# Second half of an out-projection as seven block products for eight, and the first half's last tiles in two sweeps

## The chip, the cores and the metric

The kernel runs on one core of a Trainium2 chip. The metric is the device time of one launch in microseconds (us). Engines are called by their names in the profile: PE is TensorE (PEld its weight loads), DVE is VectorE, ACT is ScalarE, POOL is GpSimd, SP the queue that issues the transfers.

## What is computed

A block of a bidirectional state-space model on 1024 tokens of 1024 channels: norm, in-projection, convolution, a scan over chunks of 128 tokens in both directions, a gate, a norm by groups, and then the out-projection with the residual and a last norm. Only the last lines matter here:

```python
    y = (yg.reshape(b, l, D_INNER) * norm_w.astype(jnp.float32)).astype(u.dtype)   # (1, 1024, 2048)
    return y @ w_out                                                               # w_out (2048, 1024)
...
        h = h + out
    return rmsnorm(h, final_norm_w)
```

All is float32. The kernel makes each float32 product out of three faster matmuls: both operands are split into a high part (rounded to the engine's reduced float32) and a low part (what is left), and high x high, high x low and low x high are added up in PSUM.

## The kernel before

Eight groups of channels go through in-projection and scan one after the other; `y` is written to DRAM (`y_d`), transposed. The out-projection contracts over 2048 channels in two halves of eight k-tiles of 128 channels (`NO` = 8). The first half can begin before the last group's scan has ended: token tiles 0 to 3 (`out_unit(0, t, ...)`) are put between the steps of the last scan, tiles 4 to 7 follow behind it. Its result plus the input x goes to DRAM (`h_d`). The second half then takes the eight token tiles once more, with `h` loaded from `h_d`; then comes the last norm.

For a token tile `out_unit` issues 48 matmuls of 128x512: eight k-tiles, three part products, two halves of the output columns. `out_prep` loads the tile of `y` (tag `th`, two buffers) and of `h` (tag `xc`, three buffers) and splits `y`: high part on ScalarE, low part on VectorE. It stands in the middle of the tile before. `load_wo` loads one row of 128 channels of the weight, 512 KB, into `raw` (tag of the pool `wp`, two buffers), scales it by the norm's weight and splits it in the same two operations (line 520 on ScalarE, 521 on VectorE). The second half's eight rows are loaded between tiles 4 to 7, two behind each, into a pool `op2` that is opened where the scan's pool is closed.

The last tile is computed in three column parts one after the other, so that its norm can begin early.

The order on each engine is set by a scheduler of the tile framework, by priorities that follow the order of the code; each engine then works through its list in that order, and waits where an operand or a buffer is not ready. All transfers here are issued by SP, in the order of its list.

```python
        raw = wp.tile([P, DM], F32, tag="raw", name=f"wo{half}{k}", bufs=2)
        nc.sync.dma_start(out=raw, in_=w_out[:, half * NO + k, :])
...
    for t in range(NC // 2, NC):
        prep = out_unit(0, t, wo1, prep, (0, t + 1) if t < NC - 1 else (1, 0))
        for _ in range(2):
            if len(wo2) % 4 == 0:
                tiles = wo_tiles(op2, 1, len(wo2) // 4)
            wo2.append(load_wo(tiles, 1, len(wo2)))
    for t in range(NC):
        prep = out_unit(1, t, wo2, prep, (1, t + 1) if t < NC - 1 else None)
```

## Time and profile before

| | us |
|---|---|
| median of 3 runs | 983.37 (981.67 to 983.98) |
| the profiled execution, device time | 985.42 |
| its span, first to last instruction | 983.7 |
| TensorE matmuls busy | 945.5 (96%) |
| VectorE busy | 727.9 (74%) |
| ScalarE busy | 539.2 (55%) |

The profile is of one execution. Times in it count from the start of its span. A list of instructions gives for each its start and its length; matmuls are pipelined, so their pace is read from the distance of starts. The first half's tiles 4 to 7 and the second half fill the last 143 us or so. A chain of waits is the work that ended last, followed back from the end.

### The profile page before, as it was taken

Reading aid. Unit: us, or ns where it says so; the run is one execution under the profiler, and the core shown is the slowest. Engines: PE = TensorE matmul, PEld = TensorE weight load, DVE = VectorE, ACT = ScalarE, POOL = GpSimd, SP = SyncE. Lnnn points to the kernel's source line nnn. Section 1 sums busy time; section 2 is a strip of 40 time slices with the busy share of each in tenths; the row PEclk is TensorE's granted clock in tenths of the full one; section 3 lists DMA queues with packets and bytes.
Section 4 is the critical chain, followed back from the end, with each engine's and each line's share of the span. In section 5 each row is a group of like instructions: output and inputs, shape, how many; then the busy total and the mean of one; then the engine's idle time right before and its main releaser. Section 6 shows DMA issues by size and latency. Waiting matters only on the chain.

```text
span 983.7 us, 15133 instructions
## 1 busy us (share of the span) xinstructions
PE 945.5 (96%) x5220; PEld 806.1 (82%) x5220; DVE 727.9 (74%) x1552; ACT 539.2 (55%) x1458; POOL 53.8 (5%) x88
## 2 busy tenths in 40 slices
...
GB/s 223 95 86 97 43 70 94 111 70 70 101 120 53 74 99 124 49 75 98 126 52 82 86 129 63 78 80 126 96 64 142 172 264 174 200 278 142 118 85 65
DMA packets 157325, 107.62 MB, mean 109 GB/s; under 512 B 75248, under 2 KB 133312, under 8 KB 157248
## 3 DMA queue, kind: packets, MB, share of 16 engines
...
## 4 chain that ended last, share of the span: by engine, by line
PE 56%; DVE 12%; DMA 12%; ACT 12%; issue 6%; POOL 2%; SPq 1%; DVEq 0%; POOLq 0%; ACTq 0%
PE po L562 16%; PE ipx L180 12%; PE ipC L180 9%; DMA fb<-rows_d 7%; PE ipB L180 7%; ACT yo L479 3%; DVE x L196 3%; ACT fb L424 2%; PE pz L157 2%; PE pyo L462 2%; PE pyd L468 2%; PE sb L393 2%; ACT fb L419 2%; DVE mt L429 1%; PE sf L393 1%
## 5 line engine op out<-in xcount | busy, mean ns | idle before, releaser
L479 ACT ACTIVATE yo<-pyo,ecs 128x64 f32<-128x64 f32 x448 | 103.1, 320 | 35.8 <-PE pyo L462 30.2
L419 ACT ACTIVATE fb<-fb,cfb 128x128 f32<-128x128 f32 x256 | 85.1, 399 | 55.1 <-DMA fb<-rows_d 49.6
L424 ACT ACTIVATE fb<-fb,cfb 128x128 f32<-128x128 f32 x256 | 84.0, 398 | 3.8 <-DVE fb L421 3.7
L196 DVE SCALAR_TENSOR_TENSOR x<-ipx,prm,x 128x1022 f32<-128x1022 f32 (+1 forms) x64 | 81.1, 1268 | 3.7 <-ACT x L190 3.6
L157 PE MATMUL pz<-wz_1l,uh 128*128 128x256 f32 (+1 forms) x248 | 73.0, 294 | 2.0 <-DVE wz_1l L123 2.0
L157 PE MATMUL pz<-wz_0h,ul 128*128 128x256 f32 (+1 forms) x248 | 73.3, 296 | 0.4 <-DVE ul L301 0.2
L157 PE MATMUL pz<-wz_0l,uh 128*128 128x256 f32 (+1 forms) x248 | 72.0, 290 | 0.0
L157 PE MATMUL pz<-wz_0h,uh 128*128 128x256 f32 (+1 forms) x248 | 71.2, 287 | 0.0
L157 PE MATMUL pz<-wz_1h,ul 128*128 128x256 f32 (+1 forms) x248 | 70.9, 286 | 0.0
L468 PEld LDWEIGHTS pyd<-xb,mt 128*128 128x128 f32 x512 | 66.7, 191 | 4.9 <-DVE mt L429 1.8
L157 PE MATMUL pz<-wz_1h,uh 128*128 128x256 f32 (+1 forms) x248 | 70.4, 284 | 0.0
L471 DVE SCALAR_TENSOR_TENSOR y<-xb,coef,pyd 128x64 f32<-128x64 f32 x256 | 62.5, 273 | 10.5 <-PE pyd L468 10.3
L468 PE MATMUL pyd<-xb,mt 128*128 128x64 f32 x512 | 64.7, 269 | 0.0
L429 DVE TENSOR_TENSOR mt<-fb,pcb 128x512 f32<-128x512 f32 x64 | 43.1, 681 | 15.3 <-PE pcb L427 13.0
L385 DVE TENSOR_TENSOR pb<-pb,sb 128x256 f32<-128x256 f32 x48 | 19.8, 412 | 42.0 <-PE sb L393 41.1
L421 DVE COPY_PREDICATED fb<-trif,fb 128x512 f32<-128x512 uint32 x64 | 47.1, 736 | 3.7 <-ACT fb L419 3.6
L157 PEld LDWEIGHTS pz<-wz_1l,uh 128*128 128x128 f32 x248 | 46.9, 189 | 3.4 <-DVE wz_1l L123 3.2
L157 PEld LDWEIGHTS pz<-wz_0h,ul 128*128 128x128 f32 x248 | 47.2, 190 | 1.3 <-DVE ul L301 1.1
L571 DVE TENSOR_TENSOR h<-po,h 128x1024 f32<-128x1024 f32 (+2 forms) x10 | 10.1, 1011 | 51.3 <-PE po L562 51.3
L157 PEld LDWEIGHTS pz<-wz_0h,uh 128*128 128x128 f32 x248 | 47.1, 190 | 0.5
L157 PEld LDWEIGHTS pz<-wz_0l,uh 128*128 128x128 f32 x248 | 47.1, 190 | 0.0
L157 PEld LDWEIGHTS pz<-wz_1h,ul 128*128 128x128 f32 x248 | 46.9, 189 | 0.2
(511 smaller groups left out, 2667.5 us busy)
## 6 DMA issues: line engine op xcount, KB each, us to landing
fb<-rows_d SPq DMA_DIRECT2D x128, 256.0 KB, 4.3
y_d<-yt SPq DMA_DIRECT2D x256, 32.0 KB, 2.0
wo<-in_ssd_w_out_dram SPq DMA_DIRECT2D x16, 512.0 KB, 4.2
yt<-y_d SPq DMA_DIRECT2D x16, 512.0 KB, 5.1
xt<-in_x_dram SPq DMA_DIRECT2D x8, 512.0 KB, 5.9
h<-in_x_dram SPq DMA_DIRECT2D x8, 512.0 KB, 4.8
h_d<-h SPq DMA_DIRECT2D x8, 512.0 KB, 3.0
h<-h_d SPq DMA_DIRECT2D x8, 512.0 KB, 3.6
```

The source lines that it names most:

```text
L157: nc.tensor.matmul(pz[:, i, 0:m], a[:, k, tok], b, start=at == 0, stop=at == 3 * NK - 1)
L180: nc.tensor.matmul(ps[:, half * 512:(half + 1) * 512], a[:, k, :], b[:, k, :], start=n == 0, stop=n == 3 * NK - 1)
L196: nc.vector.scalar_tensor_tensor(out=acc[:, o], in0=ps[:, i], scalar=w(k), in1=acc[:, o], op0=ALU.mult, op1=ALU.add)
L393: nc.tensor.matmul(ps[:, 0:CW], xb[:, CW:CW + P], xw, start=True, stop=True)
L419: nc.scalar.activation(out=ef[:, h], in_=ef[:, h], func=AF.Identity, bias=cfb[:, 1, c, hsl(g, h)])
L421: nc.vector.copy_predicated(ef, trif.bitcast(U32).unsqueeze(1).broadcast_to([P, HG, P]), fb[:, 0])
L424: nc.scalar.activation(out=ef[:, h], in_=ef[:, h], func=AF.Exp, bias=cfb[:, 0, c, hsl(g, h)])
L429: nc.vector.tensor_tensor(out=mt, in0=ef, in1=pcb[:, 0:P].unsqueeze(1).broadcast_to([P, HG, P]), op=ALU.mult)
L468: nc.tensor.matmul(pyd[:, cs], mt[:, h, :], xb[:, cs], start=True, stop=True)
L471: nc.vector.scalar_tensor_tensor(out=y[:, cs], in0=xb[:, cs], scalar=coef[:, h:h + 1], in1=pyd[:, cs], op0=ALU.mult, op1=ALU.add)
L479: nc.scalar.activation(out=yo[:, cs], in_=pyo[:, d * CW + h * HD:d * CW + (h + 1) * HD], func=AF.Copy, scale=ecs[:, d, c, hsl(g, h)])
L562: nc.tensor.matmul(pos[i], l_, r_[:, cols[i]], start=k == 0 and a == 0, stop=k == NO - 1 and a == 2)
```

## The change

The second half's product is cut into blocks: for a pair of token tiles the left operand is a 2x2 block matrix (two tiles of tokens; the first and the last four k-tiles of the half), and so is the weight (first and last four k-tiles; columns 0 to 511 and 512 to 1023). Winograd's form of Strassen's method gives the 2x2 product of blocks by seven block products in place of eight, with sums of blocks ahead of and behind them. A block product is 12 matmuls of 128x512 (`product`, line 689).

- `weights_a`, `weights_b` and `weights_c` make the seven weight operands: `w11`, `t1`, `t2`, `w21` (a), `w22`, `t3` (b), `t4` (c). `weights_a(k)` and `weights_b(k)` each load the rows k and k + 4 into `raw` and scale them on ScalarE in place (line 600); so each row is loaded twice. The differences are made on VectorE (line 610), the splits by a cast on ScalarE and a difference on VectorE (lines 591 and 592). `weights_c` needs no load.
- `pair_prep` loads both tiles of `y` and of `h` and makes the seven token operands: `a11`, `s1`, `s2`, `a12`, `s3`, `s4`, `a22`.
- `pair_unit` issues the seven products. Some of the sums behind them are made by letting a product go on in an accumulator: ScalarE copies c12 to c11, later c12 to c22 and c22 to c21, and the next products add to the copies. The product s1 x t1 is added to `h` of both tiles by VectorE.
- Tiles 4 to 7 of the first half are computed in two sweeps: all four over the k-tiles 0 to 3, then all four over 4 to 7. After the first sweep the first half's weights of the k-tiles 0 to 3 are no longer needed, and `t3` and `w22` take their place. `weights_a(n)` stands behind the n-th tile of the first sweep, `weights_b(n)` behind the n-th of the second. `x` is loaded in the second sweep (`load_h`).
- The last tile is no longer computed in column parts; its norm's second part is scaled on ScalarE and multiplied by the norm's weight on VectorE behind that.

```diff
+    def load_h(t):
+        h = cp.tile([P, DM], F32, tag="xc", name=f"h0{t}", bufs=3)
+        nc.sync.dma_start(out=h, in_=x[t * P:(t + 1) * P, :])
+        return h
...
-        h = cp.tile([P, DM], F32, tag="xc", name=f"h{half}{t}", bufs=3)
-        nc.sync.dma_start(out=h, in_=(x if half == 0 else h_d)[tok, :])
+        h = load_h(t) if t < NC // 2 else None
...
-        last = half == 1 and t == NC - 1
-        cols = [slice(0, 512), slice(512, 1024)]
-        ka = [(k, a) for k in range(NO) for a in range(3)]
...
+    def split(src, dst):
+        nc.scalar.copy(dst[0], src)
+        nc.vector.tensor_tensor(out=dst[1], in0=src, in1=dst[0].bitcast(F32), op=ALU.subtract)
+    def scaled_rows(k, name):
+        rows = []
+        for n in (k, k + HK):
+            raw = wp.tile([P, DM], F32, tag="raw", name=f"{name}{n}", bufs=2)
+            nc.sync.dma_start(out=raw, in_=w_out[:, NO + n, :])
+            nc.scalar.activation(out=raw, in_=raw, func=AF.Copy,
+                                 scale=prm[:, 192 + NO + n:193 + NO + n])
+            rows += [raw[:, 0:512], raw[:, 512:1024]]
+        return rows
...
+    def temps(name):
+        t_ = cp.tile([P, 2, 512], F32, tag="th", name=name)
+        return t_[:, 0], t_[:, 1]
...
+    def weights_a(k):
...
+        r11, r12, r21, r22 = scaled_rows(k, "wa")
+        d1, d2 = temps(f"da{k}")
+        split(r11, [p_[:, k] for p_ in W["w11"]])
+        minus(d1, r12, r11)
+        split(d1, [p_[:, k] for p_ in W["t1"]])
+        minus(d2, r22, d1)
+        split(d2, [p_[:, k] for p_ in W["t2"]])
+        split(r21, [p_[:, k] for p_ in W["w21"]])
...
+    def weights_b(k):
...
+        r11, r12, r21, r22 = scaled_rows(k, "wb")
+        d3, _ = temps(f"db{k}")
+        split(r22, [p_[:, k] for p_ in W["w22"]])
+        minus(d3, r22, r12)
+        split(d3, [p_[:, k] for p_ in W["t3"]])
...
+    def weights_c(k):
...
+        e, d = temps(f"dc{k}")
+        for o, n in ((e, 0), (d, 1)):
+            minus(o, W["w21"][n][:, k].bitcast(F32), W["t2"][n][:, k].bitcast(F32))
+        nc.vector.tensor_tensor(out=d, in0=d, in1=e, op=ALU.add)
+        split(d, [p_[:, k] for p_ in W["t4"]])
...
+    def pair_prep(i):
+        ys, hs = [], []
+        for t in (2 * i, 2 * i + 1):
+            yt = cp.tile([P, NO, P], F32, tag="th", name=f"yt1{t}")
+            nc.sync.dma_start(out=yt, in_=y_v[:, NO:2 * NO, t * P:(t + 1) * P])
+            ys.append([yt[:, q * HK:(q + 1) * HK].rearrange("p k t -> p (k t)") for q in range(2)])
+        for t in (2 * i, 2 * i + 1):
+            h = cp.tile([P, DM], F32, tag="xc", name=f"h1{t}", bufs=3)
+            nc.sync.dma_start(out=h, in_=h_d[t * P:(t + 1) * P, :])
+            hs.append(h)
...
+        put("a11", a11)
+        s1, s2 = room("a")
+        nc.vector.tensor_tensor(out=s1, in0=a21, in1=a22, op=ALU.add)
+        put("s1", s1)
+        minus(s2, s1, a11)
+        put("s2", s2)
+        put("a12", a12)
+        s3, s4 = room("b")
+        minus(s3, a11, a21)
+        put("s3", s3)
+        minus(s4, a12, s2)
+        put("s4", s4)
+        put("a22", a22)
+        return A, hs
+    def product(ps, a, w, fresh):
+        n = 0
+        for k in range(HK):
+            for l_, r_ in ((a[0], w[0]), (a[0], w[1]), (a[1], w[0])):
+                nc.tensor.matmul(ps, l_[:, k, :], r_[:, k, :], start=fresh and n == 0,
+                                 stop=n == 3 * HK - 1, skip_group_check=True)
+                n += 1
...
+            nc.scalar.activation(out=h[:, HI], in_=h[:, HI], func=AF.Copy, scale=r)
+            nc.vector.tensor_tensor(out=h[:, HI], in0=h[:, HI], in1=fnw[:, HI], op=ALU.mult)
+            nc.sync.dma_start(out=out[t * P:(t + 1) * P, HI], in_=h[:, HI])
...
+    def add(t, h, cs, ps, ss, i):
+        nc.vector.tensor_tensor(out=h[:, cs], in0=ps, in1=h[:, cs], op=ALU.add)
+        nc.scalar.activation(out=ps, in_=h[:, cs], func=AF.Square, accum_out=ss[:, i:i + 1])
+        if i:
+            nc.vector.tensor_tensor(out=ss[:, 0:1], in0=ss[:, 0:1], in1=ss[:, 1:2], op=ALU.add)
...
+    def pair_unit(i, prep, nxt):
+        A, (h1, h2) = prep
+        c1 = ps_ip.tile([P, DM], F32, tag="ip", name=f"po1{i}")
+        c11, c12 = c1[:, LO], c1[:, HI]
+        product(c12, A["a11"], W["w11"], True)
+        nc.scalar.copy(c11, c12)
+        pw = pst(f"p5{i}")
+        product(pw, A["s1"], W["t1"], True)
+        for h in (h1, h2):
+            nc.vector.tensor_tensor(out=h[:, HI], in0=pw, in1=h[:, HI], op=ALU.add)
+        product(c12, A["s2"], W["t2"], False)
+        product(c11, A["a12"], W["w21"], False)
+        nprep = pair_prep(nxt) if nxt is not None else None
+        c2 = ps_ip.tile([P, DM], F32, tag="ip", name=f"po2{i}")
+        c21, c22 = c2[:, LO], c2[:, HI]
+        nc.scalar.copy(c22, c12)
+        ss1, ss2 = (ops.tile([P, 3], F32, tag="ss", name=f"oss{i}_{j}") for j in range(2))
+        add(2 * i, h1, LO, c11, ss1, 0)
+        product(c22, A["s3"], W["t3"], False)
+        product(c12, A["s4"], W["w22"], False)
+        nc.scalar.copy(c21, c22)
+        add(2 * i + 1, h2, HI, c22, ss2, 0)
+        add(2 * i, h1, HI, c12, ss1, 1)
+        product(c21, A["a22"], W["t4"], False)
+        finish(2 * i, h1, ss1, False)
+        add(2 * i + 1, h2, LO, c21, ss2, 1)
+        finish(2 * i + 1, h2, ss2, nxt is None)
+        return nprep
...
+    tiles, pos = list(range(NC // 2, NC)), {}
+    preps = {tiles[0]: prep}
+    for q in range(2):
+        for n, t in enumerate(tiles):
+            if q == 0:
+                if n:
+                    preps[t] = out_prep(0, t)
+                if n < 2:
+                    po = ps_ip.tile([P, DM], F32, tag="ip", name=f"po0{t}")
+                    pos[t] = [po[:, cs] for cs in (LO, HI)]
+                else:
+                    pos[t] = [pst(f"po0{t}_{c}") for c in range(2)]
+            _, yh, yl = preps[t]
+            for k in range(q * HK, (q + 1) * HK):
+                for a in range(3):
+                    for p_, cs in zip(pos[t], (LO, HI)):
+                        nc.tensor.matmul(p_, (yh, yh, yl)[a][:, k, :], wo1[k][(0, 1, 0)[a]][:, cs],
+                                         start=k == 0 and a == 0, stop=k == NO - 1 and a == 2)
+            if q == 0:
+                weights_a(n)
+            else:
+                h = load_h(t)
+                for p_, cs in zip(pos[t], (LO, HI)):
+                    nc.vector.tensor_tensor(out=h[:, cs], in0=p_, in1=h[:, cs], op=ALU.add)
+                nc.sync.dma_start(out=h_d[t * P:(t + 1) * P, :], in_=h)
+                weights_b(n)
...
-    for t in range(NC // 2, NC):
-        prep = out_unit(0, t, wo1, prep, (0, t + 1) if t < NC - 1 else (1, 0))
-        for _ in range(2):
-            if len(wo2) % 4 == 0:
-                tiles = wo_tiles(op2, 1, len(wo2) // 4)
-            wo2.append(load_wo(tiles, 1, len(wo2)))
-    for t in range(NC):
-        prep = out_unit(1, t, wo2, prep, (1, t + 1) if t < NC - 1 else None)
+    prep = pair_prep(0)
+    for k in range(HK):
+        weights_c(k)
+    for i in range(NC // 2):
+        prep = pair_unit(i, prep, i + 1 if i + 1 < NC // 2 else None)
```

How the instructions stand on three engines is shown by pieces of their lists (no times are in them). A name ends in the buffer's number; `wo1h0`, `wo1l0` are the second half's weights of before, high and low part, `po04` is the accumulator of the first half's tile 4, `yh06` the high part of tile 6's `y`.

VectorE, where tile 5's sum is added to `h`, before (line 565 adds, 521 makes a weight's low part, 538 that of `y`):

```order
L521 SCALAR_TENSOR_TENSOR wo1l0_9314<-wo10_9315,prm_74,wo1h0_9313 128x1024 [waits DMAHW3_49,DMAHW2_49,DMAHW4_49,DMAHW1_49,Activation_49]
L521 SCALAR_TENSOR_TENSOR wo1l0_9314<-wo11_9319,prm_74,wo1h0_9313 128x1024 [waits Activation_49]
L565 TENSOR_TENSOR h05_9281<-po05_9323,h05_9281 128x1024 [waits PE_49]
L538 TENSOR_TENSOR yl11_9556<-yt11_9551,yh11_9555 128x1024 [waits DMAHW7_49,Activation_49]
L521 SCALAR_TENSOR_TENSOR wo1l0_9314<-wo12_9382,prm_74,wo1h0_9313 128x1024 [waits DMAHW0_49,Activation_49]
L521 SCALAR_TENSOR_TENSOR wo1l0_9314<-wo13_9386,prm_74,wo1h0_9313 128x1024 [waits DMAHW1_49,Activation_49]
```

and after (774 adds half a tile, 610 and 592 belong to `weights_a(0)` and `(1)`, 542 is the low part of `y`):

```order
L592 TENSOR_TENSOR ow21_9278<-wa4_9282,ow21_9278 128x512 [waits Activation_49]
L774 TENSOR_TENSOR h04_9466<-po04_9250,h04_9466 128x512 [waits PE_49]
L774 TENSOR_TENSOR h04_9466<-po04_9250,h04_9466 128x512
L610 TENSOR_TENSOR da1_9333<-wa1_9327 128x512 [waits Activation_49]
L774 TENSOR_TENSOR h05_9509<-po05_9302,h05_9509 128x512 [waits PE_49]
L592 TENSOR_TENSOR ow11_9275<-wa1_9327,ow11_9275 128x512 [waits Activation_49]
L610 TENSOR_TENSOR da1_9333<-wa5_9330,da1_9333 128x512 [waits DVE_49,Activation_49]
L592 TENSOR_TENSOR ot1_9276<-da1_9333,ot1_9276 128x512 [waits Activation_49]
L592 TENSOR_TENSOR ow21_9278<-wa5_9330,ow21_9278 128x512 [waits Activation_49]
L592 TENSOR_TENSOR ot2_9277<-da1_9333,ot2_9277 128x512 [waits Activation_49]
L774 TENSOR_TENSOR h05_9509<-po05_9302,h05_9509 128x512
L542 TENSOR_TENSOR yl06_9347<-yt06_9344,yh06_9346 128x1024 [waits DMAHW4_49,Activation_49]
```

Behind the add of tile 5 there now stands the low part of row 1 (`wa1`), and the low part of tile 6's `y` stands behind all of `weights_a(1)`.

ScalarE, from the last weights to the first token operands of the second half, before (the last four rows and tiles 2 to 4):

```order
L537 CAST yh12_9621<-yt12_9617 128x1024 [waits DMAHW6_49,PE_49]
L520 ACTIVATE wo1h1_9449<-wo15_9455,prm_74 128x1024 [waits DMAHW5_49]
L520 ACTIVATE wo1h1_9449<-wo16_9518,prm_74 128x1024 [waits DMAHW0_49]
L520 ACTIVATE wo1h1_9449<-wo17_9522,prm_74 128x1024 [waits DMAHW1_49]
L537 CAST yh13_9687<-yt13_9683 128x1024 [waits DMAHW3_49,PE_49,Activation_49]
L537 CAST yh14_9753<-yt14_9749 128x1024 [waits DMAHW3_49,DVE_49,PE_49]
```

and after (600 scales a loaded row, 591 casts; `yh0_a11` holds the first pair's a11 and s1):

```order
L600 ACTIVATE wb2_9555<-wb2_9555,prm_74 128x1024 [waits DMAHW3_49]
L600 ACTIVATE wb6_9558<-wb6_9558,prm_74 128x1024 [waits DMAHW4_49,DVE_49]
L591 CAST ow22_9472<-wb6_9558 128x512 [waits Activation_49]
L591 CAST ot3_9471<-db2_9561 128x512 [waits DVE_49]
L600 ACTIVATE wb3_9596<-wb3_9596,prm_74 128x1024 [waits DMAHW7_49]
L600 ACTIVATE wb7_9599<-wb7_9599,prm_74 128x1024 [waits DMAHW0_49,DVE_49]
L591 CAST ow22_9472<-wb7_9599 128x512 [waits Activation_49]
L591 CAST ot3_9471<-db3_9602 128x512 [waits DVE_49]
L591 CAST yh0_a11_9618<-yt10_9610 128x512 [waits DMAHW1_49]
L591 CAST yh0_s2_9627<-yt10_9610 128x512
L591 CAST yh0_a11_9618<-sa_0_9622 128x512 [waits DVE_49]
L591 CAST yh0_s2_9627<-sa_0_9622 128x512 [waits DVE_49]
```

The first pair's token casts stand behind the last cast of `weights_b(3)`; before, those of the first tiles stood between and ahead of the weights.

TensorE between two tiles of the second half, before (tiles 2 and 3):

```order
L562 MATMUL po12_9658<-wo1h1_9449,yh12_9621 128x512 x2
L562 MATMUL po12_9658<-wo1l1_9450,yh12_9621 128x512 x2
L562 MATMUL po12_9658<-wo1h1_9449,yl12_9622 128x512 x2
L562 MATMUL po13_9724<-wo1h0_9313,yh13_9687 128x512 [waits Activation_49]
L562 MATMUL po13_9724<-wo1h0_9313,yh13_9687 128x512
L562 MATMUL po13_9724<-wo1l0_9314,yh13_9687 128x512 x2
```

and after, in the second pair, from its fourth product to its fifth (`p52` is the third pair's second product, `po21` the second pair's c2):

```order
L693 MATMUL po11_9823<-ow21_9278,yh1_s2_9741 128x512 x2
L693 MATMUL po11_9823<-ow21_9278,yl1_s2_9742 128x512
L693 MATMUL p52_9989<-ot1_9276,yh2_a11_9884 128x512 [waits Activation_49]
L693 MATMUL p52_9989<-ot1_9276,yh2_a11_9884 128x512
L693 MATMUL p52_9989<-ot1_9276,yl2_a11_9885 128x512 [waits DVE_49]
L693 MATMUL p52_9989<-ot1_9276,yh2_a11_9884 128x512 x2
L693 MATMUL p52_9989<-ot1_9276,yl2_a11_9885 128x512
L693 MATMUL p52_9989<-ot1_9276,yh2_a11_9884 128x512
L693 MATMUL po21_9912<-ot3_9471,yh1_s3_9749 128x512 [waits Activation_49]
L693 MATMUL po21_9912<-ot3_9471,yh1_s3_9749 128x512
```

Seven matmuls of the third pair's second product, with its token operand and that one's low part, have been put ahead of the second pair's fifth product.

## Rows read from the trace of the kernel before

**Rows 1.** The chain of waits from 850 us: start, length, what.

```profile
849.91 127.26 PE po L562 x569
```

**Rows 2.** The list of TensorE's instructions (start, length, what), and line 562's groups.

```profile
948.91 0.63 PE L562 MATMUL po<-wo1h,yh 128*128 128x512 f32 x2
949.38 0.63 PE L562 MATMUL po<-wo1l,yh 128*128 128x512 f32 x2
...
L562 PEld LDWEIGHTS po<-wo1h,yh x136: 187/188/189, 887.1 to 976.5; 128*128 128x128 f32 x136
L562 PE MATMUL po<-wo1h,yh x136: 274/392/398, 887.3 to 976.6; 128*128 128x512 f32 x120, 128*128 128x256 f32 x16
```

**Rows 3.** The lists of SP, ScalarE and VectorE between tiles 4 and 7.

```profile
861.89 1.52 SPq L517 DMA_DIRECT2D wo<-in_ssd_w_out_dram  x2
869.87 1.58 SPq L517 DMA_DIRECT2D wo<-in_ssd_w_out_dram  x2
878.76 1.53 SPq L517 DMA_DIRECT2D wo<-in_ssd_w_out_dram  x2
...
859.39 2.19 ACT L520 ACTIVATE wo1h<-wo,prm 128x1024 fp32r<-128x1024 f32 x2 [4.89 <-DMA y_d<-yt]
867.37 2.40 ACT L520 ACTIVATE wo1h<-wo,prm 128x1024 fp32r<-128x1024 f32 x2 [1.67 <-DMA wo<-in_ssd_w_out_dram]
874.40 1.15 ACT L520 ACTIVATE wo1h<-wo,prm 128x1024 fp32r<-128x1024 f32 x1 [4.62 <-DMA wo<-in_ssd_w_out_dram]
882.41 1.15 ACT L520 ACTIVATE wo1h<-wo,prm 128x1024 fp32r<-128x1024 f32 x1 [4.46 <-DMA wo<-in_ssd_w_out_dram]
...
860.58 2.48 DVE L521 SCALAR_TENSOR_TENSOR wo1l<-wo,prm,wo1h 128x1024 fp32r<-128x1024 f32 x2 [3.98 <-ACT wo1h L520]
865.11 1.23 DVE L565 TENSOR_TENSOR h<-po,h 128x1024 f32<-128x1024 f32 x1 [2.06 <-PE po L562]
```

**Rows 4.** Busy time by stretch: stretch, its length, PE, PEld, DVE, ACT, POOL, clock, DMA.

```profile
860.00:870.00 10.00, 10.00 (x44) 8.07 (x43) 6.28 (x6) 4.94 (x5) 0.00 (x0) 1.00 0.94 318
```

**Rows 5.** The list of VectorE and ScalarE in the last tile.

```profile
971.51 0.69 DVE L571 TENSOR_TENSOR h<-po,h 128x512 f32<-128x512 f32 x1 [0.93 <-PE po L562]
972.24 0.60 ACT L572 ACTIVATE po<-h 128x512 f32<-128x512 f32 x1 [3.85 <-DVE h L571]
...
977.20 0.42 DVE L571 TENSOR_TENSOR h<-po,h 128x256 f32<-128x256 f32 x1 [1.35 <-PE po L562]
977.66 0.39 ACT L572 ACTIVATE po<-h 128x256 f32<-128x256 f32 x1 [2.34 <-DVE h L571]
```

**Rows 6.** Transfers from 840 us (count, KB, median us to landing); landing of all weight rows.

```profile
yt<-y_d SPq DMA_DIRECT2D x9, 512.0 KB, 4.5
wo<-in_ssd_w_out_dram SPq DMA_DIRECT2D x6, 512.0 KB, 5.3
...
DMA to landing us min/median/max: 3.5/4.2/5.9
```

**Rows 7.** TensorE's list at the beginning, and a stretch at the end (columns as Rows 4).

```profile
14.34 0.47 PE L157 MATMUL pz<-wz_0h,uh 128*128 128x320 f32 x1
14.61 0.47 PE L157 MATMUL pz<-wz_0l,uh 128*128 128x320 f32 x1
...
17.03 0.31 PE L157 MATMUL pz<-wz_1h,uh 128*128 128x320 f32 x1
17.18 0.31 PE L157 MATMUL pz<-wz_1l,uh 128*128 128x320 f32 x1
...
982.00:983.00 1.00, 0.00 (x0) 0.00 (x0) 0.00 (x0) 0.00 (x0) 0.00 (x0) 0.68 0.34 125
```

89 lines of the change are left out of this document (49 added, 40 removed).

## The prediction, made before the changed kernel was run

> **What bounds it now.** I read the chain of waits first, for the stretch from 850 us to the end. From 849.91 us on it is one piece, 127.26 us of the 569 matmuls of line 562 [rows 1]: TensorE never waits in the whole out-projection, so a matmul taken away there shortens the run, and a new wait of TensorE lengthens it. The list of instructions gives the pace: two pairs of 128x512 matmuls start at 948.91 and 949.38, so one takes 0.467 / 2 = 0.233 us, and its weight load of 0.188 us lies beside it [rows 2]. The second half begins at 887.3 [rows 2], the last matmul has ended at 977.16 (849.91 + 127.26), and the span ends at 983.7. A token tile has 48 such matmuls, 11.2 us.
>
> Then I looked at what feeds the second half's weights. `raw` has two buffers, so a weight row can only be fetched once the row two before it has been read out. Before, the pairs of loads are issued at 861.89, 869.87 and 878.76, each as soon as VectorE has made the low parts, and ScalarE starts on the pairs at 859.39, 867.37, 874.40 and 882.41 [rows 3]: 7.0 to 8.0 us per pair. That is a round trip and no rate: ScalarE and VectorE are busy for 4.94 and 6.28 us of 10 in the stretch from 860 to 870 [rows 4]. Only three round trips are needed, and 37 us of first-half matmuls (849.91 to 887.3) lie over them, so they fit.
>
> **What goes.** Seven products of 12 matmuls for a pair of tiles replace 96 matmuls by 84: 384 become 336 in all (the 48 half-wide ones of the last tile count as 24). 48 x 0.233 = 11.2 us of TensorE, all of it on the path.
>
> **What comes, the weights.** Before: eight row loads. After: each of the eight rows twice, 16 loads, through the same two buffers: one pair before the state-space part ends, then seven round trips instead of three. With them come 28 casts and 16 scalings on ScalarE (28 x 0.60 + 16 x 1.15 = 35 us) and 52 VectorE operations 512 wide. One of these takes 0.69 alone [rows 5]; the 1024 wide one takes 1.23 [rows 3], so I take 0.65 for one in a row of several. Both engines have room for this; the latency is the matter. The order of the instructions (second pair of fences in the section on the change) shows that ScalarE casts the first pair's token operands only behind the last cast of `weights_b(3)`, and TensorE's first product needs those. So I walk along that chain.
>
> The walk starts where VectorE stands. Its add of tile 5 stands ahead of the low part of row 1, and waits for tile 5's last matmul, which comes at the same place in the matmul order as before, so the add starts at 865.1 [rows 3]. Add and low part, 2 x 0.65: the buffer is free at 866.4, the next load goes out at 866.5. A load landed 4.2 us after its issue in the median of the program's 16 and 5.3 in the median of the last six [rows 6]; I take 4.7.
> Row 2: load 4.7, scaling 1.15 [rows 3], cast 0.60 [rows 5], low part 0.65, handing over 0.2: 873.8.
> Row 3: 4.7 + 2.6 as well for the first of its two rows; the second is scaled, split and read out 2.7 later, VectorE having six operations to do: 883.8.
> `weights_b(0)`, second row: 4.7 + 1.15 + a difference 0.7: 890.4.
> `weights_b(1)` and `(2)`: each 4.7 + 1.15 + 1.15 + 0.7 + 0.1 = 7.8: 906.0.
> `weights_b(3)` to the first token cast: 4.7 + 2.3 + 0.7 + 2 x 0.60 = 8.9: **914.9**.
> The chain holds six loads. The first of a pair took from 3.65 us (878.76 to 882.41) to 5.5 (861.89 to 867.37) [rows 3], so this point lies between 908.6 and 919.7. On SP's queue the loads of x, the stores of h and the loads of y now stand between the weight loads; in the walk each of them is through before the weight load behind it has its buffer. If instead the tiles' pool opened at 859.4 as before and not earlier, row 1 ends 1.5 us later; that lies within.
>
> TensorE could have been there at 887.3. In the two sweeps it stalls too: `yh06` is cast behind row 1 at 868.8, its low part comes at 870.9, tile 7's operands at 876.9 and 878.1. Together 6.7 us, so the sweeps end at 894.0 in place of 887.3. This costs nothing, since TensorE then waits until 914.9 anyway; were the chain short, it would be 6.7 us.
>
> **What comes, the pairs.** 28 products x 12 x 0.233 = 78.4 us. Waits inside: the first pair's second token tile can only be loaded when `weights_b(3)` has left its `th` buffer, 0.4 us after the first product began; with 4.5 us for such a load [rows 6] and a sum, a cast and a low part behind it, the first three products are 4.4 us late. Then ScalarE copies c12 into c22 behind two casts of `t4`, 1.7 us late. In the second pair the first product waits until ScalarE has squared the old accumulator, behind five casts and a load: 2.8 us. Then the scheduler has put part of the third pair's second product ahead of the fifth (last fence), and ScalarE's copy for the fifth stands behind four casts for the third pair: 2.2 us. Sum 11.1, and 0.2 in the third pair: 11.3 us. No row shows such waits of TensorE; below I keep 5 (the token load alone), above 16 (the waits of the second pair in the third and fourth as well), and take the walk. TensorE ends at 914.9 + 78.4 + 11.3 = 1004.6.
>
> **The end.** Before, 6.5 us from the last matmul to the end. After, the last add and square are 512 wide in place of 256: 0.69 for 0.42 and 0.60 for 0.39 (0.39 and 0.42 are the same operations at half the width) [rows 5]; the product with the norm weight stands behind the scaling, + 0.7, and one such product of 0.4 no longer stands ahead. + 0.8: 7.3 us, and the span ends at 1011.9.
>
> **Sum.** Against the profiled span of 983.7: start of the second half + 27.6, matmuls and stalls in it - 11.2 + 11.3 (about zero), end + 0.8: + 28 us. The profiled execution itself took 985.42 us with its span of 983.7; the median of the runs is 983.37. I add the 28 us to the median: 1011.6.
>
> **Rivals.** *The matmuls saved are kept* (faster): if the seven round trips ended before 887.3, the result is 983.4 - 11.2 + 0.8 and some 5 us of waits in the pairs: 978. This decides if the remaining six loads take (887.3 - 866.5) / 6 = 3.5 us each with all work between them; the rows show 7.0 to 8.0 for a pair with less work between. For it speaks only that the added loads may overlap better. *A quicker chain:* 3.65 us for every load and 5 us of waits give 999. *The clock:* at the program's beginning, 128x320 matmuls start 0.27 us apart at 14.34 and 14.61 and 0.15 apart at 17.03 and 17.18, and behind the last matmul the recorded clock falls from 1.00 to 0.68 in the stretch from 982 to 983 [rows 7], that is from 2.4 towards 1.2 GHz, 5 us after TensorE fell idle. The new gap is 20 us, so the first products may run at the lower level; at the beginning that lasted until 16.2. Two products of 2.8 us at 0.15/0.27 of the speed are 4.5 us longer. The first two products wait for token operands for 4.4 us in any case, so most of it is hidden; taken at 0, at most + 4.5, which with the slow chain (919.7) and 16 us of waits gives 1026.
> The Trainium skill, "TensorE: Matmul & The Clock Gate", section "HAM oscillation — how this bites in real kernels", speaks against this change: a wait for a transfer between groups of matmuls puts TensorE back to the half rate, and the next group starts cold. By that rule the 4.5 us would be paid at least once; the trace agrees that the clock falls behind the last matmul, and shows no gap of that length between matmuls. *No change:* a chain that ends near 888 to 890 by chance; no row speaks for it.
>
> **How the numbers follow.** Forecast, the chain holds the second half up: 0.80, 1001 to 1021 (early start 908.6 with stalls of 7, up to 919.7 with 15). Quicker chain 0.07. Lower clock or more stalls, above 1021, 0.07. Faster 0.04. No change 0.02. A measurement of this kernel can tell about 0.2% (2 us) from nothing. The first three are all slower: 0.94. The range of 1001 to 1021 holds 0.8.
>
> **What would show it.** Right: line 693's first matmul starts between 908 and 920, TensorE idle before it for about 20 us and released by ScalarE; ScalarE's idle time ahead of line 600 ended by the weight loads; 336 matmuls of line 693 at 0.233 us; about 11 us of TensorE waits inside the pairs; 7.3 us behind the last matmul. Wrong: a first product before 895, or ScalarE or VectorE busy without gaps from 865 to 915, so that a rate and no round trip holds it.

## The result, and the profile after

The changed kernel takes 1012.23 us (median of 4 runs, 1010.77 to 1013.5), the kernel before 983.06 us beside it (981.67 to 983.98): a ratio of 1.0297, with a 95% interval of 1.0279 to 1.0316. It is 29 us slower, and the prediction (1011.6, 1001 to 1021) holds it. The profiled span is 1010.5 us, 26.8 more than before.

First a selection of TensorE's instructions: the longest waits from the sweeps on, and two places where the pace is back behind one (start, length, engine and line, operation, and in brackets the idle time ahead of it with what ended it). They answer to [rows 1] and [rows 2], where TensorE never waits:

```profile
866.18 1.22 PE L767 MATMUL po<-wo0h,yh 128*128 128x512 f32 x2 [3.58 <-ACT yh L541]
...
912.91 1.22 PE L693 MATMUL po<-ow,yh_a 128*128 128x512 f32 x2 [21.13 <-ACT yh_a L591]
...
916.83 0.62 PE L693 MATMUL po<-ow,yh_a 128*128 128x512 f32 x2
...
928.53 0.73 PE L693 MATMUL po<-ot,yh_s 128*128 128x512 f32 x2 [0.78 <-ACT po L735]
...
934.22 1.22 PE L693 MATMUL po<-ow,yh_s 128*128 128x512 f32 x2 [2.64 <-ACT po L716]
...
936.95 0.74 PE L693 MATMUL po<-ow,yh_s 128*128 128x512 f32 x2
...
1002.14 0.40 PE L693 MATMUL po<-ot,yl_a 128*128 128x512 f32 x1
```

TensorE stands still for 21.1 us ahead of the first product, at 912.91; before, the second half began at 887.3 [rows 2]. From there to the last matmul's end, 1002.5, it is 89.6 us, where the kernel before took 89.9 (887.3 to 977.16) for 384 matmuls in place of 336. So both of the prediction's findings are there: the second half starts late, and the 48 matmuls saved bring next to nothing.

What ended the 21 us stands in ScalarE's list (line 600 scales a loaded row, line 591 casts), in one row of VectorE's (line 610, the last reading of the buffer that is loaded next) and in SP's (issues of loads; line 655 loads `h`); they answer to [rows 3]:

```profile
883.84 1.16 ACT L600 ACTIVATE wb<-wb,prm 128x1024 f32<-128x1024 f32 x1 [2.54 <-DMA wb<-in_ssd_w_out_dram]
...
891.05 1.15 ACT L600 ACTIVATE wb<-wb,prm 128x1024 f32<-128x1024 f32 x1 [2.76 <-DMA wb<-in_ssd_w_out_dram]
...
899.84 1.15 ACT L600 ACTIVATE wb<-wb,prm 128x1024 f32<-128x1024 f32 x1 [4.65 <-DMA wb<-in_ssd_w_out_dram]
901.85 1.15 ACT L600 ACTIVATE wb<-wb,prm 128x1024 f32<-128x1024 f32 x1 [0.86 <-DMA wb<-in_ssd_w_out_dram]
903.03 0.62 ACT L591 CAST ow<-wb 128x512 fp32r<-128x512 f32 x1
...
908.39 1.15 ACT L600 ACTIVATE wb<-wb,prm 128x1024 f32<-128x1024 f32 x1 [4.02 <-DMA wb<-in_ssd_w_out_dram]
...
912.25 0.61 ACT L591 CAST yh_a<-yt 128x512 fp32r<-128x512 f32 x1
```

```profile
903.03 0.69 DVE L610 TENSOR_TENSOR db<-wb,wb 128x512 f32<-128x512 f32 x1 [6.64 <-ACT wb L600]
```

```profile
894.32 0.33 SPq L655 DMA_DIRECT2D h<-h_d  x1
894.75 0.84 SPq L599 DMA_DIRECT2D wb<-in_ssd_w_out_dram  x2
...
903.04 0.33 SPq L655 DMA_DIRECT2D h<-h_d  x1
903.75 0.98 SPq L599 DMA_DIRECT2D wb<-in_ssd_w_out_dram  x2
```

Read the last two pairs of loads together. The last pair goes out from 903.75 on, right when VectorE has read out the first buffer (903.03 + 0.69 = 903.72); the row lands and is scaled at 908.39; ScalarE has idled for 4.0 us. From pair to pair it is 7.2, 8.8 and 8.6 us (883.84, 891.05, 899.84, 908.39). ScalarE's waits for these eight loads come to 16.3 us. The first token cast stands behind the last of them, at 912.25.

SP's list holds a second wait at the same place. Ahead of each of these two pairs stands a load of `h`, which waits until the store of that `h` has landed: 3.9 us to 894.32 and 6.6 us to 903.04. It is out at 894.65 where the first pair's buffer comes free at 894.53, and at 903.37 where the second's does at 903.72. So the buffers and SP's list hold these two pairs at nearly the same moment, and as far as these rows show either alone would have held them almost as long. The two pairs before them (883.84 and 891.05) have no such load of `h` between them.

The same by stretch: PE, its weight loads, DVE, ACT and POOL busy, the granted clock, DMA share, GB/s; it answers to [rows 4]:

```profile
890.00:900.00 10.00, 1.78 (x8) 1.12 (x6) 3.27 (x6) 3.69 (x5) 0.00 (x0) 0.81 0.77 253
900.00:910.00 10.00, 0.00 (x0) 0.00 (x0) 2.03 (x3) 4.70 (x6) 0.00 (x0) 0.50 0.76 272
910.00:920.00 10.00, 5.95 (x16) 4.07 (x17) 6.22 (x10) 4.91 (x9) 0.00 (x0) 0.66 0.24 68
```

From 890 to 910 no engine works half of the time. The granted clock falls to 0.50, TensorE's lower level (1.2 GHz), while it idles, and the first matmuls behind the gap run at it.

### The profile page after: what moved, and what is told of

Same layout as the page of the kernel before. It is cut to its first block, busy times and chain, and to the rows that moved or that the text cites. A ratio compares the mean times of both kernels' runs of the same rounds, so it can differ in the third digit from the quotient of the medians.

```text
span 1010.5 us, 15211 instructions
## 1 busy us (share of the span) xinstructions
PE 942.3 (93%) x5148; PEld 798.4 (79%) x5148; DVE 774.3 (77%) x1654; ACT 580.2 (57%) x1538; POOL 55.2 (5%) x88
## 4 chain that ended last, share of the span: by engine, by line
PE 47%; DMA 17%; DVE 15%; ACT 12%; issue 6%; POOL 2%; SPq 1%; DVEq 0%; POOLq 0%; ACTq 0%
PE ipx L180 11%; PE ipC L180 9%; DMA fb<-rows_d 8%; PE ipB L180 7%; PE po L693 4%; ACT yo L479 3%; DVE x L196 2%; PE po L767 2%; PE pz L157 2%; PE po L555 2%; ACT fb L424 2%; DMA wb<-in_ssd_w_out_dram 2%; PE pyo L462 2%; PE pyd L468 2%; PE sb L393 2%
## 5 line engine op out<-in xcount | busy, mean ns | idle before, releaser
L157 PEld LDWEIGHTS pz<-wz_1h,uh 128*128 128x128 f32 x248 | 46.8, 189 | 0.0
```

Source lines behind the costliest of these rows:

```text
L157: nc.tensor.matmul(pz[:, i, 0:m], a[:, k, tok], b, start=at == 0, stop=at == 3 * NK - 1)
```

## Experiments

Each ratio is against the kernel before, run beside it (981.8 to 984.9 us there). "First" and "last" are the start of the first product and the end of the last matmul in the profile, "stage" the time between them, in us. In the kernel before the stage is 89.9 us; seven products without any wait would be 78.4.

| run | time | ratio (95% interval) | first | last | stage |
|---|---|---|---|---|---|
| changed kernel | 1012.23 | 1.0297 (1.0279 to 1.0316) | 912.9 | 1002.5 | 89.6 |
| e1 four raw buffers | 995.31 | 1.0146 (1.0121 to 1.0171) | 894.0 | 986.1 | 92.1 |
| e2 half rows | 999.84 | 1.0178 (1.0161 to 1.0195) | 898.3 | 991.6 | 93.4 |
| e3 no second load | 1002.63 | 1.0210 (1.0195 to 1.0225) | 907.7 | 992.9 | 85.3 |
| e4 gap filled | 1015.96 | 1.0341 (1.0321 to 1.0360) | 913.5 | 1006.9 | 93.4 |
| e5 eight products | 1022.18 | 1.0381 (1.0368 to 1.0394) | 914.8 | 1012.1 | 97.3 |
| e6 sweeps alone | 983.07 | 0.9987 (0.9975 to 0.9999) | - | - | - |
| e7 rows once | 989.28 | 1.0050 (1.0035 to 1.0066) | 888.4 | 983.1 | 94.7 |
| e8 rows once, GpSimd | 997.46 | 1.0130 (1.0116 to 1.0145) | 884.9 | 986.6 | 101.8 |
| e9 own banks | 1011.15 | 1.0265 (1.0250 to 1.0281) | 915.5 | 1002.1 | 86.6 |
| e10 rows once, banks | 985.32 | 1.0004 (0.9993 to 1.0015) | 887.5 | 975.4 | 87.9 |
| e11 the same, tokens early | 984.29 | 0.9995 (0.9985 to 1.0005) | 886.4 | 973.3 | 86.9 |
| e12 the same, all banks | 979.57 | 0.9969 (0.9957 to 0.9981) | 884.2 | 969.6 | 85.4 |

"First" and "last" count from the start of each profile, and the executions already differ ahead of the edited lines. The last group's `y_0r`, an instruction that all the kernels have, shows it, here in the kernel before and in the changed one:

```profile
719.29 0.55 POOL L85 TENSOR_TENSOR y_0r<-y_0m,neghalf 128x1 f32<-128x1 f32 x1 [39.04 <-DVE y_0m L82]
```

```profile
716.37 0.55 POOL L85 TENSOR_TENSOR y_0r<-y_0m,neghalf 128x1 f32<-128x1 f32 x1 [39.45 <-DVE y_0m L82]
```

In the other profiles it stands between 715.3 and 720.0. A difference of a few us in "first" or "last" can be this; "stage" is free of it. Counted from that instruction, the second half begins after 168.0 us in the kernel before, 196.5 in the changed kernel, 178.5 in e1, 180.5 in e2, 190.5 in e3, and between 167.5 and 169.5 in e6 to e8 and e10 to e12. The second half is thus 28.5 us late in the changed kernel, and at most 1.4 us from e6 on, e9 excepted.

### What makes the second half late: round trips, a rate, or the transfers?

**e1, four raw buffers**

```diff
+            far = nraw[0] // 2 % 2 == 1
+            nraw[0] += 1
-            raw = wp.tile([P, DM], F32, tag="raw", name=f"{name}{n}", bufs=2)
+            raw = (op2 if far else wp).tile([P, DM], F32, tag="raw2" if far else "raw",
+                                            name=f"{name}{n}", bufs=2)
...
-    fnw = op2.tile([P, DM], F32, name="fnw")
+    fnw = up.tile([P, 4, DM], F32, tag="ul1", name="fnw")[:, 0, :]
```

> Edit: the rows for weights_a and weights_b go through four buffers in place of two (two more in op2; the final norm's weight moves to a tile that is free behind the sweeps). Loads and arithmetic stay the same. Theory A, latency of round trips through two raw buffers: the last three pairs of loads lie beside the work on the pairs before them, so each costs about 3.5 us of ScalarE (2 x 1.15 + 2 x 0.60) in place of 8 to 9, and the y tile's load behind tile 7's store sets the first product: line 693 starts at about 898 to 901 in place of 912.9; time about 999. Rival B, the rate of ScalarE and VectorE: no change, 1012. Rival C, the transfers' rate: 11.6 MB moved from 860 to 910 at the 272 GB/s of the fullest stretch take 43 us in place of 50: first product at about 905, time about 1005, and the stretches before it at 0.75 or more of the DMA share.

995.31 us, 17 less (15 by the ratios), with every load and every operation still there, and better than theory A's 999. The first product comes at 893.99, 19 us earlier than in the changed kernel and 4 to 7 earlier than expected. TensorE's first product (its row names nothing that it waited for), the stretch ahead of it and ScalarE's cast for it:

```profile
893.99 1.19 PE L698 MATMUL po<-ow,yh_a 128*128 128x512 f32 x2 [8.36 <-issue]
```

```profile
880.00:890.00 10.00, 5.63 (x25) 4.19 (x23) 6.93 (x12) 7.10 (x9) 0.00 (x0) 0.99 0.97 319
```

```profile
893.27 0.62 ACT L591 CAST yh_a<-yt 128x512 fp32r<-128x512 f32 x1 [3.44 <-DMA yt<-y_d]
```

A rate of ScalarE or VectorE is out: the same work ends earlier as soon as more loads may be under way. The transfers' rate was not the bound of the changed kernel either, which moved 253 and 272 GB/s in the two stretches of its gap; here it is 319 GB/s at a DMA share of 0.97 (and the kernel before had 318 in one stretch, [rows 4]). In e1 it may well be the next bound. The first product comes when ScalarE's cast has ended (893.89), and the cast waited for the first y tile, 3.4 us longer than for anything else.

Two more things moved with this edit. The load of the final norm's weight went from 851.35 to 885.20, and the first weight rows from 852.75 to 849.50, which may be up to 3 us of the 19. And the loads of `h`, which stood in SP's list ahead of two pairs of weight loads, stand behind all of them here, and in e2 too. So whether more buffers would do the same with SP's list as it was, no run here tells.

**e2, half rows.** `weights_b` uses only the right halves of its rows.

```diff
-        r11, r12, r21, r22 = scaled_rows(k, "wb")
+        raw = wp.tile([P, 2, 512], F32, tag="raw", name=f"wb{k}", bufs=2)
+        for j, n in enumerate((k, k + HK)):
+            nc.sync.dma_start(out=raw[:, j], in_=w_out[:, NO + n, 512:1024])
+            nc.scalar.activation(out=raw[:, j], in_=raw[:, j], func=AF.Copy,
+                                 scale=prm[:, 192 + NO + n:193 + NO + n])
+        r12, r22 = raw[:, 0], raw[:, 1]
```

> Edit: weights_b loads only columns 512 to 1023 of its two rows (all that it uses) into one raw buffer, so two weights_b can be under way; still two raw buffers; 2 MB less is moved, and eight scalings are 512 wide and not 1024. Theory A, round trips: the four trips of weights_b become two of about 8 us: first product at about 901, time about 1001. Rival B, rate: only ScalarE's 8 x 0.55 = 4.4 us less: time about 1008. Rival C, transfers' rate: 2 MB at 272 GB/s = 7.7 us less: 905, time about 1004.5.

999.84 us, where theory A gave 1001 and the rivals 1004.5 and 1008. The first product starts at 898.3, 2.7 us earlier than expected, and the stage is 3.8 us longer than in the changed kernel. Half the trips take away 16 of the 28.5 us.

**e3, no second load**

```diff
-        r11, r12, r21, r22 = scaled_rows(k, "wb")
-        d3, _ = temps(f"db{k}")
-        split(r22, [p_[:, k] for p_ in W["w22"]])
-        minus(d3, r22, r12)
-        split(d3, [p_[:, k] for p_ in W["t3"]])
+        for n, op in (("t3", ALU.subtract), ("w22", ALU.add)):
+            e, d = temps(f"d{n}{k}")
+            for o, q in ((e, 0), (d, 1)):
+                nc.vector.tensor_tensor(out=o, in0=W["t2"][q][:, k].bitcast(F32),
+                                        in1=W[("t1", "w11")[n == "t3"]][q][:, k].bitcast(F32), op=op)
+            nc.vector.tensor_tensor(out=d, in0=d, in1=e, op=ALU.add)
+            split(d, [p_[:, k] for p_ in W[n]])
```

> Edit: weights_b loads nothing; t3 is made as t2 - w11 and w22 as t2 + t1, high and low parts apart on VectorE (24 sums in place of 4), and ScalarE's eight scalings for it go. Theory A, round trips: the chain of loads ends with weights_a(3) at about 880; what is left is VectorE work, 32 operations of 0.65 = 21 us, about half of it in VectorE's idle time before 890: first product at about 900, time about 1000, now held by VectorE without gaps. Rival B, rate already now: 20 more VectorE operations, 13 us, less 5 on ScalarE: time about 1020. Rival C, transfers' rate: 4 MB less, 15 us: time about 997 with VectorE idle in places.

1002.63 us, near theory A's 1000 and far from rival B's 1020, but not in the parts that were expected: the first product comes at 907.7 and not at 900, and the stage is shorter, 85.3 us. Rival C's 997 is not far either, but it had VectorE idle in places. By stretch (behind its length the busy time of TensorE, its weight loads, VectorE, ScalarE), with ScalarE's cast for the first product:

```profile
880.00:890.00 10.00, 10.00 (x45) 8.04 (x44) 9.96 (x18) 3.29 (x6) 0.00 (x0) 1.00 0.06 24
890.00:900.00 10.00, 1.98 (x9) 1.26 (x7) 10.00 (x17) 1.85 (x3) 0.00 (x0) 0.73 0.44 157
```

```profile
907.00 0.62 ACT L591 CAST yh_a<-yt 128x512 fp32r<-128x512 f32 x1 [4.23 <-DMA yt<-y_d]
```

Up to 903.5 VectorE is the bound: it has no gap from 880 to 900, and the DMA share is 0.06 and then 0.44. The weights' latency is gone and a rate has taken its place. What stands last ahead of the first product is again one load: the y tile's goes out at 902.75, when VectorE has left its buffer, and ScalarE waits 4.2 us for it.

### Is the lower clock a cost of its own?

**e4, gap filled**

```diff
+    pg = pst("fill")
+    for _ in range(88):
+        nc.tensor.matmul(pg, wo1[4][1][:, 0:P], wo1[5][1][:, 0:512], start=True, stop=True)
     prep = pair_prep(0)
```

> Edit: the changed kernel with 88 added 128x512 matmuls (88 x 0.233 = 20.5 us, their product is never read) between the sweeps and the first product, so that TensorE is busy in the gap from 891.4 to 912.9. Theory A: waits for operands cover the slower first products; 0 to -2 us: 1010 to 1012. Rival D, the lower clock behind the gap costs time of its own: the granted clock of 0.66 from 910 to 920 becomes 1.00 and the time falls by 4.5 us or more: 1007.7 or less.

```profile
910.00:920.00 10.00, 6.00 (x23) 3.66 (x21) 5.39 (x9) 4.76 (x8) 0.00 (x0) 1.00 0.24 71
```

```profile
913.51 0.74 PE L693 MATMUL po<-ow,yh_a 128*128 128x512 f32 x2 [1.58 <-ACT yh_a L591]
...
919.24 0.73 PE L693 MATMUL p<-ot,yh_a 128*128 128x512 f32 x2 [2.33 <-ACT yh_a L591]
920.39 0.79 PE L693 MATMUL p<-ot,yl_a 128*128 128x512 f32 x1 [0.42 <-DVE yl_a L592]
...
936.94 0.98 PE L693 MATMUL po<-ow,yh_s 128*128 128x512 f32 x2 [3.21 <-ACT po L716]
```

```profile
920.00:930.00 10.00, 9.60 (x34) 7.41 (x34) 9.37 (x16) 2.67 (x5) 0.00 (x0) 0.83 0.00 0
```

The clock in the stretch from 910 to 920 is 1.00 in place of 0.66, and nothing is gained: 1015.96 us, 4 more, which neither theory had. The second product starts at 919.24 (918.41 in the changed kernel), held by the second y tile, on which VectorE starts at 917.84 (917.01). A faster first product only waits longer in front of it, here 2.33 us. So the lower clock at the first product costs nothing by itself, as the prediction had it.

But the run doesn't take the lower clock away, it moves it. Behind that wait the second product falls to half the pace: the seven matmuls from 920.39 to 923.54 take 3.15 us where 7 x 0.233 is 1.63, and the clock of that stretch is 0.83. There it is paid: the start of the third product is 2.3 us later than in the changed kernel (924.27 and 922.00), where that of the second is 0.8 later. Some 1.5 of the 4 us are this. Another 0.6 comes at the sixth product (2.7 us later; the fifth is 2.1 later): ScalarE's copy for the fifth product stands ahead of the second cast of `t4` in its list, and VectorE waits 1.8 us for that cast. The rest is 0.6 ahead of the first product and some 1.5 us in the second pair, with waits of 0.66 and 1.00 us. What the whole of the lower clock costs this run does not price.

### Do the matmuls saved count, and do the sweeps cost?

**e5, eight products**

```diff
+        product(pst(f"x{i}"), A["a11"], W["w11"], True)
         pw = pst(f"p5{i}")
```

> Edit: the changed kernel with an eighth product for each pair (a11 x w11 once more, into a bank that is never read): 384 matmuls behind the first half in place of 336. Theory A, a matmul taken away inside the pairs shortens the run by its 0.233 us: 48 x 0.233 = 11.2 us more, less 1 to 2 us where the second and sixth product wait for operands anyway: time about 1022. Rival B, the pairs are held by ScalarE and VectorE: only the third and fourth pair, which have no waits, get longer: 24 x 0.233 = 5.6 us, about 1018 or less.

1022.18 us, 9.95 more by the medians, 8.3 by the ratios (0.0084 x 983), against 10 expected by A and 5.6 by B; the ratios are the better measure, since the kernel before beside it was 1.5 us slower too. The stage grows by 7.7 us (97.3 to 89.6), and TensorE's waits in it shrink: one of 2.5 us and one of 0.7 are left, 3.2 in place of 5.7.

```profile
914.82 1.22 PE L693 MATMUL po<-ow,yh_a 128*128 128x512 f32 x2 [21.41 <-ACT yh_a L591]
933.66 1.22 PE L693 MATMUL po<-ot,yh_s 128*128 128x512 f32 x2 [2.47 <-ACT po L736]
```

A matmul counts for some 70 to 75% of its 0.233 us (7.7 and 8.3 of 11.2); the rest falls into waits that were there.

**e6, sweeps alone.** The two sweeps stay; behind them stands the second half of the kernel before, and one of its row loads behind each tile of a sweep.

```diff
-            if q == 0:
-                weights_a(n)
-            else:
+            if q == 1:
...
-                weights_b(n)
+            if len(wo2) % 4 == 0:
+                wt = wo_tiles(op2, 1, len(wo2) // 4)
+            wo2.append(load_wo(wt, 1, len(wo2)))
```

> Edit: the two sweeps of the changed kernel with the second half of the kernel before (96 matmuls for two tiles, eight row loads, one behind each tile of a sweep). Theory A: eight loads through two buffers fit beside the sweeps (three round trips of 8 us in 37 us); the sweeps cost the wait for yh06's cast of about 3.6 us and no more: 982 to 986. Rival B, the two sweeps are the cost (operands of all four tiles ahead of time, banks held): the 6.7 us of the walk and what comes behind, 989 or more.

983.07 us, 0.9987 of the kernel before: the sweeps are free, and even the wait of 3.6 us that the changed kernel has inside them (866.18) is not there. The second half follows the first without a gap:

```profile
887.41 0.62 PE L694 MATMUL po<-wo0h,yl 128*128 128x512 f32 x2
887.87 0.63 PE L595 MATMUL po<-wo1h,yh 128*128 128x512 f32 x2
```

### What it takes to keep the gain

**e7, rows once.** Each row is loaded once, through four buffers. From the second pair of rows on, the first sweep has left the room of `t3` and `w22`, so that all six operands can be made from one load.

```diff
+    def weights(k, R, also):
+        r11, r12, r21, r22 = R
+        split(r11, [p_[:, k] for p_ in W["w11"]])
+        split(r21, [p_[:, k] for p_ in W["w21"]])
+        if also:
+            split(r22, [p_[:, k] for p_ in W["w22"]])
+        minus(r11, r12, r11)
+        split(r11, [p_[:, k] for p_ in W["t1"]])
+        if also:
+            minus(r21, r22, r12)
+            split(r21, [p_[:, k] for p_ in W["t3"]])
+        minus(r22, r22, r11)
+        split(r22, [p_[:, k] for p_ in W["t2"]])
```

> Edit: each weight row is loaded once, through four raw buffers: for the rows 1 to 3 and 5 to 7, t3 and w22 are made from the same loaded rows as w11, t1, t2 and w21, since the first sweep has by then left their room; for rows 0 and 4 they are made as t2 - w11 and t2 + t1. Differences are made in place, so the y tiles of the first pair load early. Theory A, round trips: the weights are through at about 890; VectorE has 28 to 35 us of weight work between 852 and 890; first product at 890 to 894; 78.4 us of matmuls and about 8 us of waits, the end 9 us behind: about 987. Rival B, the pairs' own cost keeps it above 995 even with the first product at 894, as with four raw buffers.

989.28 us, the first product at 888.4, 24.5 us earlier than in the changed kernel. The profiled execution took 992.81, the longest of the six, and was behind from the beginning (`y_0r` at 720.02): counted from there the lateness is gone to within 1 us, and the stage (94.7 us) shows what it holds, with waits of 3.1 and 3.9 us as the largest:

```profile
892.10 0.50 PE L688 MATMUL po<-ow,yl_a 128*128 128x512 f32 x1 [3.09 <-DVE yl_a L592]
...
912.20 0.73 PE L688 MATMUL po<-ow,yh_s 128*128 128x512 f32 x2 [3.86 <-ACT po L711]
```

**e8, sums for t4 on GpSimd** (in `weights_c`, the three sums for each k)

```diff
-            nc.vector.tensor_tensor(...)
+            nc.gpsimd.tensor_tensor(...)
```

> Edit: as the run with rows loaded once, and the 12 sums for t4 go from VectorE to GpSimd. Theory A: VectorE has 12 x 0.65 = 7.8 us less in the first pair, where the squares and copies for the seventh product and the second pair wait for its sums; those waits shrink by some 4 us: about 983. Rival B: GpSimd's sums take over 1.5 us each and t4 itself comes late: no gain or 987 to 990.

997.46 us, 8 more than e7: worse than either theory. A 128x512 sum takes GpSimd 1.3 to 1.7 us by the profile (VectorE 0.69), and ScalarE's copy for the fifth product (line 730) stands in its list behind casts that need these sums:

```profile
893.86 3.24 POOL L631 TENSOR_TENSOR dt<-ow,ot 128x512 f32<-128x512 f32 x2 [47.58 <-DVE sb L595]
897.18 1.62 POOL L633 TENSOR_TENSOR dt<-dt 128x512 f32<-128x512 f32 x1
```

```profile
911.55 0.62 ACT L591 CAST ot<-dt 128x512 fp32r<-128x512 f32 x1 [3.61 <-POOL dt L633]
912.07 0.58 ACT L730 COPY po<-po 128x512 f32<-128x512 f32 x1
```

```profile
912.71 1.22 PE L688 MATMUL po<-ot,yh_s 128*128 128x512 f32 x2 [12.95 <-ACT po L730]
```

**e9, own banks: c11 and c12 in a tile each** (the changed kernel otherwise)

```diff
-        c1 = ps_ip.tile([P, DM], F32, tag="ip", name=f"po1{i}")
-        c11, c12 = c1[:, LO], c1[:, HI]
+        c12, c11 = pst(f"c12{i}"), pst(f"c11{i}")
```

> Edit: the changed kernel with c11 and c12 in two tiles of one PSUM bank each in place of one tile of two banks; nothing else. Theory A: the sixth product of a pair writes c12 and waited for ScalarE's square, which writes into c11 of the same tile (2.6 us at 934.2 in the changed kernel), and at the start of the next pair for the squares again; these waits go: 3 to 5 us less, about 1008. Rival B: the operands of the sixth product (the sums, VectorE without a gap there) would hold it at the same place: no change, 1012.

The stage is 86.6 us, 3.0 less, as expected: the sixth product no longer waits for the square. A wait of 2.1 us appears one product later, for the square of c22, which still shares a tile with c21 (e12 takes that away). The time falls by 1.1 us only (3.1 by the ratios, whose intervals just overlap): in the profiled execution the first product came 2.6 us later, 0.8 of it ahead of the edited lines and the rest in the weight loads, which the edit doesn't explain. The place of the wait is shown, its gain only in the stage.

```profile
938.21 1.22 PE L693 MATMUL po<-ot,yh_a 128*128 128x512 f32 x2 [2.09 <-ACT po L716]
```

The Trainium skill, "Perfetto Trace Analysis", section "Matmuls", says that independent groups of matmuls should go through different PSUM banks, so that what empties one lies beside the next group. The rows do not test that rule by itself: the edit gives c11 and c12, the two halves of one tile before, a tile each, and the wait went with the shared tile.

**e10, rows once with own banks, and e11, in which the first pair's token operands come ahead of the last weight row's**

```diff
-                if n < 3:
+                if n < 2:
...
+                else:
+                    R[3] = R.get(3) or rows(3)
...
     prep = pair_prep(0)
+    weights(3, R[3], True)
```

> Edit: rows loaded once as before, and c11 and c12 in a bank each. Theory A: the waits of 3.9 and 0.8 us for squares go from the pairs: 989.3 - 4.7 = about 984.5. Rival B: VectorE, which has no gap from 888 to 923, holds the seventh product and the second pair at the same place: 988 to 989.

> Edit: rows loaded once, a bank each for c11 and c12, and the first pair's token operands are made ahead of the last weight row's on ScalarE and VectorE. Theory A: the 3.1 us that the first product waits for its low part behind weight work go too: about 981.5. Rival B: the same VectorE work stands a little later in front of the next product: 984 to 986.

985.32 and 984.29 us: both cannot be told from the kernel before (1.0004 and 0.9995). Theory A's 984.5 holds for e10; for e11 its 981.5 was too low, and the time lies in rival B's range. Between the two no difference is shown. In e11 the second half starts at 886.4 with no gap ahead, and this is what is left:

```profile
890.08 0.50 PE L688 MATMUL c<-ow,yh_a 128*128 128x512 f32 x1 [1.22 <-DVE ow L592]
899.97 0.73 PE L688 MATMUL po<-ot,yh_s 128*128 128x512 f32 x2 [0.66 <-ACT po L729]
909.85 0.89 PE L688 MATMUL po<-ot,yh_a 128*128 128x512 f32 x2 [4.02 <-ACT po L711]
```

**e12, c21 and c22 in a tile each as well**

```diff
-        c2 = ps_ip.tile([P, DM], F32, tag="ip", name=f"po2{i}")
-        c21, c22 = c2[:, LO], c2[:, HI]
+        c22, c21 = (ps_ip.tile([P, DM], F32, tag="ip", name=f"{n}{i}")[:, LO] for n in ("c22", "c21"))
```

> Edit: as the run with the token operands made early, and c22 and c21 as well in a tile (and bank) each. Theory A: the one wait left inside the pairs, 4.0 us of the first pair's seventh product for the square of c22 in the tile that it shares with c21, goes; t4's last low part, ready at 908.4 and used by the last three matmuls alone, costs about 1 us of it: 3 us less, and the 2 us that the lower clock took behind that wait: 984.3 - 4 = about 980, below the kernel before (982 to 985). Rival B: t4's parts hold the seventh product at the same place: 983 to 984, no change against the kernel before.

979.57 us, as theory A had it, 0.9969 (0.9957 to 0.9981) of the kernel before: 3 us faster than it. The seventh product now waits 0.3 us for `t4`'s low part; the next wait is the second pair's first product's, for its y tile.

```profile
906.41 0.50 PE L688 MATMUL c<-ot,yh_a 128*128 128x512 f32 x1 [0.27 <-DVE ot L592]
908.68 0.73 PE L688 MATMUL c<-ow,yh_a 128*128 128x512 f32 x2 [1.53 <-ACT yh_a L591]
```

Of the 11.2 us of matmuls saved, 4.5 arrive in the stage (89.9 to 85.4), and the end behind the last matmul takes back 1.5 of them (6.5 to 8.0). The first pair still holds waits, a slower stretch behind them (granted clock 0.83), and VectorE with hardly a gap:

```profile
890.00:900.00 10.00, 9.34 (x40) 7.06 (x39) 9.85 (x17) 3.18 (x6) 0.00 (x0) 1.00 0.24 80
900.00:910.00 10.00, 8.20 (x34) 5.72 (x33) 9.50 (x17) 5.66 (x13) 0.00 (x0) 1.00 0.38 106
910.00:920.00 10.00, 10.00 (x37) 7.62 (x36) 8.50 (x17) 4.56 (x10) 1.48 (x2) 0.83 0.39 109
```

## Why the prediction was right, point by point

| step | predicted | changed kernel |
|---|---|---|
| add of tile 5; next load issued | 865.1; 866.5 | 862.64; 863.96 |
| second row of `weights_b(0)` through | 890.4 | 887.7 |
| `weights_b(2)` through | 906.0 | 903.8 |
| TensorE idle until the first product | 20 us, 914.9 | 21.1 us, 912.91 |
| the stage, less 78.4 of matmuls | 11.3 | 11.2 (89.6 - 78.4) |
| last matmul to the end | 7.3 | 8.0 |
| span | 1011.9 | 1010.5 |

**The chain of loads** is the step on which the forecast rests, and e1 to e3 show it as a cause: more buffers, half the trips or no second load each bring the second half forward, by 18, 16 and 6 us, with the work of the engines the same, less or more; in e7, with both more buffers and one load for each row, the lateness is gone. The walk's trips of 7.8 us measured 7.2, 8.8 and 8.6. The column of the changed kernel runs 2 to 2.7 us early throughout, which is the shift between the two profiles: the changed kernel's was ahead by 2.9 us already at `y_0r`, and tile 5's last matmul by 2.5. With that taken out the walk is right to about 1 us: the second half begins 28.5 us late, and 27.6 was predicted. What the walk had only just right is SP's list: it has the loads and stores of `h` through before each buffer comes free, and in the rows the loads of `h` wait for their stores and are through just as the buffers come free (894.65 and 894.53, 903.37 and 903.72).

**The sweeps** end 6.8 us late, as predicted (6.7), but by other parts: from tile 5's last matmul to 891.8 it is 29.2 us for 96 matmuls of 22.4. One wait of 3.6 us stands in it, and the fourteen matmuls behind it (866.18 to 872.46) take 6.28 us in place of 3.26, at the lower clock. That the lateness costs nothing is right; e6 shows more, that the sweeps by themselves have no wait.

**The matmuls saved** are on the path, as assumed, for the most part: e5 gives back about 8 of 11.2 us.

**The waits in the pairs** were right as a sum by luck, and wrong as a list. The 11.3 us were waits alone. Waits of TensorE in the whole stage are 5.7 us (0.7, 0.9, 2.6, 1.5); another 3.1 (1.8 and 1.3, below) are matmuls at the lower clock, which the sum had at nothing, and the other 2.4 us no row tells apart. The square (predicted 2.8 us, for the second pair's first product) came as the sixth product's wait of 2.6 us in the first pair, because c11 and c12 share a tile, which the walk did not see; e9 shows it. The token load's 4.4 us became 1.1 of waiting, and the slower first product filled 1.8 more. The range was added up with 7 and 15 us of stalls, where the text keeps 5 and 16: with 5 its lower end would be 999, the time of one of the rivals.

**The lower clock** was taken at 0 and put among the rivals. Behind the 21 us gap nine matmuls take 3.92 us (912.91 to 916.83) where 9 x 0.233 is 2.10; the second product waits for its y tile in any case, and e4 shows that a faster first product gains nothing there. But the pace fell a second time behind the wait of 2.6 us, and there six matmuls took 2.73 us in place of 1.40 (934.22 to 936.95), with no further wait in that pair to hide it. Some 1.3 us of the stage is the clock's, then; that is an estimate from the trace, and no run tests it. The rule of "TensorE: Matmul & The Clock Gate" in the Trainium skill, section "HAM oscillation — how this bites in real kernels", is that a group of matmuls behind a wait for a transfer starts at the lower rate. The rows at 912.91 agree. The price here, the 1.3 us, is far below the 4.5 at which the rival put it. The sign that the prediction took from the program's beginning is weak: in the stretch from 14 to 16 us, where matmuls start 0.27 us apart, the granted clock of the kernel before is recorded as 1.00, so no row shows that this pace was the clock's.

**The end** was 0.7 us longer than predicted. The walk left out that VectorE finishes tile 6 (line 710) between the two last adds (line 715), as the chain of waits has it:

```profile
1002.34 1.28 DVE h L710
1003.62 0.61 DVE h L715
```

The last product is complete at 1002.5 and its add begins at 1003.62.

**The rivals.** "The matmuls saved are kept" needed trips that fit in before 887.3. e11 and e12 build that case, and even then they do not come down to the 978 of the prediction: 984.3 with c21 and c22 sharing a tile, 979.6 without. "A quicker chain" (999) is about what e1 (995.3) and e2 (999.8) come to, the one by trips that overlap and the other by fewer trips; neither has faster ones.
